# Compressed keys, values and queries as one product of 1024 columns, three of eight blocks with seven products, in one written sequence with its neighbours

## The chip, the cores and the metric

One core of one Trainium2 chip runs the whole program. The metric is the time of one execution on the device in microseconds (us). Three runs of the kernel before took 1565.64, 1566.04 and 1566.29 us, so the median is 1566.04. The execution that the profiler recorded took 1566.54 us, and its trace spans 1564.8 us. Engines are named as the profile names them: PE multiplies matrices, PEld loads its weights, DVE and ACT do the elementwise work, POOL is the third vector engine, SP issues most transfers.

## What is computed

One residual block of an encoder over 256 tokens of 2048 channels, in float32. The part that matters here is the projection of the normalised input `u` onto the columns of `w_in`, and what its compressed parts feed:

```python
def _mixer(u, positions, w_in, ...):
    proj = u @ w_in
    (r_q, r_k, r_v, r_g, c_q, c_kv, k_pe, g_ret, g_mla) = jnp.split(proj, offs, axis=-1)
    ...                                     # retention branch from r_q, r_k, r_v, r_g
    y_ret = ry @ w_ret_o
    q = (_rmsnorm(c_q, q_a_norm_g) @ w_q_b).reshape(B, S, MLA_HEADS, MLA_QK_DIM)
    q_nope, q_pe = q[..., :QK_NOPE], _rope(q[..., QK_NOPE:], positions)
    kv = (_rmsnorm(c_kv, kv_a_norm_g) @ w_kv_b).reshape(B, S, MLA_HEADS, QK_NOPE + V_HEAD)
    k_nope, v = kv[..., :QK_NOPE], kv[..., QK_NOPE:]
    k_pe = _rope(k_pe.reshape(B, S, 1, QK_ROPE), positions)
    ...                                     # block-causal attention of 16 heads
    y_mla = my.reshape(B, S, MLA_V_W) @ w_mla_o
    merged = jax.nn.sigmoid(g_ret) * y_ret + jax.nn.sigmoid(g_mla) * y_mla
    return merged @ w_out
```

`c_q` and `c_kv` have 512 columns each, `k_pe` has 64, and each gate `g_ret`, `g_mla` has 2048. After the mixer comes a feed-forward part of 8192 hidden channels, which the change leaves alone.

## The kernel before

**Numbers in two halves.** Every float32 weight and activation is split into `hi`, a rounded copy that ACT casts, and `lo`, the rest that DVE subtracts (`split`, L548 to L551, and `weights`, L162 to L170). A product then takes three matmuls: hi by hi, hi by lo and lo by hi. Each matmul has 128 by 128 weights (tokens) against up to 512 columns. All of this work, from loading (`raw` tiles, 512 KB each, a ring of five) to the cast, the subtraction and the matmuls, is a stream: SP loads, ACT and DVE prepare, PE multiplies.

**Blocks with eight and with seven products.** The large products `gr` (the gate `g_ret`), `yr` (`w_ret_o`) and `gm` (the gate `g_mla`) come from `product` (L484). Their 2048 columns are done in two halves of 1024 columns, and each half runs over eight blocks of 256 input channels (`KP` is 8). A plain block (`Eight`) has two parts of 4 products, so 24 matmuls of 512 columns. A block by Strassen's scheme in Winograd's form (`Seven`) has four parts of 2, 2, 2 and 1 products, so 21 matmuls, and DVE first builds weight sums `fa` and `fb` for it (L307, L316, L317) that also have to be split. `SEVEN` says which of the eight blocks are of this kind, for each half.

**Banks.** A half of a product fills all eight banks of PSUM: four that both kinds of block add to (`ROLE`), and four that only `Seven` blocks use. PSUM has two pools of four banks, `mmps` and `atps`; `Banks.add` gives `ROLE` banks one pool and the others the other pool, by turns from half to half. After the last `Seven` of a half `partial` (L444) folds its own four banks into `tmp` with two ACT copies and four DVE operations; after the last block `done` adds these sums to the four `ROLE` banks.

**What sets the order.** `stream` (L470) writes the order out by hand: at part n it loads up to part n+6, prepares up to part n+4, does the matmuls of part n, then calls `after(n)` and whatever stands in `later` (`soon`). Every engine takes its instructions in this order. The ring of prepared weights has six slots (four `hi`/`lo` pairs and two more). Work outside such a written sequence is ordered by an automatic scheduler.

**The stages around the change.** `gr` and `yr` are one written sequence (L894 to L906). Then, in automatic order, come `c_kv` with `k_pe` as one product of 576 columns in two pieces of 288 (tiles `kv`, `kw`, from L952) and `c_q` with 512 columns (tile `cq`, from L974), both plain. `lora_norm` squares the raw sums on ACT, takes the root on POOL and scales on DVE straight from PSUM; `lora_turn` transposes the result on PE into `cc`, cut into hi and lo. `late_turn` (L964) does the same for the key `k_pe` and turns it by its position (`rope`, L685). The second written sequence is `gm` (L992). After it the attention (tiles `lt`, `ms`, `mt`, `my`) is ordered automatically; its first products read `cc`.

Of the kernel before, what the change touches and what calls it, by code (L numbers as in the profile page):

```python
# [19 lines left out]
P = 128  # L20
S = 256
# [23 lines left out]
SEVEN = {"rv": ((2, 4, 5), (2, 4, 5)), "gr": ((3, 5), (2, 4, 5)), "yr": ((2, 4, 5), (2, 4, 5)), "gm": ((3, 5, 6), (2, 4, 5))}  # L45
# [60 lines left out]
def block_kernel(ctx: ExitStack, tc: tile.TileContext, A):  # L106
# [234 lines left out]
    class Banks:  # L341
        def __init__(self, name, half, pairs, steps):
            self.name, self.half, self.q = name, half, {}
            self.left = {f: steps for f in range(1, 8)}
            self.left[0] = 0
            for f in ROLE.values():
                self.left[f] += 2 * (pairs - steps)

        def add(self, f, a, w):
            if f not in self.q:  # L350
                self.q[f] = (mmps if (f in ROLE.values()) == (self.half == 0) else atps)(f"{self.name}{self.half}{f}")
                start = True
            else:
                start = False
# [129 lines left out]
    def product(parts, name, src, x, sets, tmp, at, done, order):  # L484
        count = sum(isinstance(p, Seven) for p, h in parts if h == 0)
        for half in range(2):
            banks = Banks(name, half, KP, len(at[half]))
# [14 lines left out]
            for m in range(KP):  # L502
# [228 lines left out]
    def tokens(out, act):  # L731
        def done(banks, t, c, col):
            o = out[:, t, col * 512 : (col + 1) * 512]
# [153 lines left out]
    yc = kp.tile([P, max(map(len, SEVEN["yr"])), 2, 4, P], F32R, name="yc")  # L887

# [4 lines left out]

    parts = product([], "gr", A["w_gret"], x, xc, tmp, SEVEN["gr"], tokens(m1, AF.Sigmoid), range(KP))  # L894
    making = iter([])

    def after(n):
# [9 lines left out]
    kctx.close()  # L907

    with ExitStack() as mctx:
        cc = big("cc", F32R, shape=(P, 2 * LT, 2, S))  # L910
        kpe = rope_pool.tile([P, S], F32, tag="kpe", bufs=1, name="kpe")
        lp = ExitStack()
        lpool = lp.enter_context(tc.tile_pool(name="lp", bufs=1))

        def lora_norm(s, parts):
            n = len(parts) // 2
            cn = lpool.tile([P, 2, LORA], F32, name=f"cn{s}")
            ss = lpool.tile([P, 2, 32], F32, name=f"ss{s}")[:, :, :n]
            for i, (t, c0, ps) in enumerate(parts):
                o = cn[:, t, c0 : c0 + ps.shape[1]]  # L920
                SC.activation(
                    o, ps, AF.Square, scale=rx[:, t : t + 1], accum_out=ss[:, t, i // 2 : i // 2 + 1]
                )
            r = lpool.tile([P, 64], F32, name=f"rc{s}")[:, :2]
            if n == 1:
                rms(r, ss[:, :, 0], LORA, 2)
            else:
                V.tensor_tensor(out=r, in0=ss[:, :, 0], in1=ss[:, :, 1], op=ALU.add)
                rms(r, r, LORA, 2)
            V.tensor_tensor(out=r, in0=r, in1=rx, op=ALU.mult)  # L930
            for t, c0, ps in parts:
                V.tensor_scalar(cn[:, t, c0 : c0 + ps.shape[1]], ps, r[:, t : t + 1], None, op0=ALU.mult)
            return cn

        def lora_turn(s, cn):
            pTs = [atps(f"lt{s}{jj}") for jj in range(2)]
            for jj, pT in enumerate(pTs):
                for j in range(2):
                    for t in range(2):
                        o = j * S + t * P  # L940
                        k = 2 * jj + j
                        PE.transpose(pT[:, o : o + P], cn[:, t, k * P : (k + 1) * P], ident)
            yield
            for jj, pT in enumerate(pTs):
                for j in range(2):
                    k = 2 * jj + j
                    g = (V_QA, V_KV)[s] + k
                    o = cc[:, LT * s + k]
                    split(o[:, 0], o[:, 1], pT[:, j * S : (j + 1) * S], scale=vec[:, g : g + 1])
            yield  # L950

        pkv = [[mmps(f"kv{t}"), mmps(f"kw{t}")] for t in range(2)]  # L952
        for k in range(0, KT, 2):
            for half in range(2):
# [3 lines left out]
        kn = lpool.tile([P, 2, 2, 64], F32, name="kn")  # L958
        for t in range(2):
            for j in range(2):  # L960
                SC.activation(kn[:, t, j], pkv[t][1][:, 224:288], AF.Copy, scale=rx[:, t : t + 1])
# [629 lines left out]
```

## Time and profile before

| what | value |
|---|---|
| time, median of three runs | 1566.04 us |
| the profiled execution: its time | 1566.54 us |
| the profiled execution: its span | 1564.8 us |
| ACT busy | 962.6 us (62%) |
| PEld busy | 1311.0 us (84%) |
| mean share of the 16 DMA engines in use, 452.4 to 500.3 us | 0.70 to 0.72 |
| granted PE clock in every stretch quoted below | 1.00 |

Engines overlap, so their busy times don't add up. The one that is never idle in a stretch sets the time of that stretch, and an engine that is idle there costs nothing. A busy PE is a modelled quantity, since matmuls are pipelined; so the pace of PE is best read as a stretch of time divided by the matmuls in it. `L357` names a line of the kernel before; the same helpers stand one to three lines further down in the changed kernel.

### The profile page before, as it was taken

The numbers are of one execution on the slowest core, as the hardware profiler recorded it, in microseconds if no ns is written. First come the engines' busy times: TensorE is split into PE (matmuls) and PEld (weight loads), VectorE is DVE, ScalarE is ACT, GpSimd is POOL, SyncE is SP. The second block draws the span as 40 slices with busy tenths as digits, with TensorE's granted clock in tenths as the row PEclk, the third lists the DMA queues.
The fourth block names the chain that finished last, engine by engine and source line by source line (L and its number), as shares of the span: only waits on it lengthen the run. The fifth ranks groups of instructions, "written<-read, shape, count | busy, mean of one in ns | idle before, by whom it ended". The sixth has DMA issues, their size and how long they took to land.

```text
span 1564.8 us, 21391 instructions
## 1 busy us (share of the span) xinstructions
PE 1551.3 (99%) x7655; PEld 1311.0 (84%) x7655; DVE 1316.0 (84%) x1787; ACT 962.6 (62%) x1416; POOL 39.3 (3%) x76
## 2 busy tenths in 40 slices
PE   9999999999999999999999999999999999999997
PEld 7888888888898888888888888888888888888886
DVE  7898877799976988976567689887978899989996
ACT  6645655566545667875445567676767766656664
POOL 0000000000000000000000000000000100000000
PEclk9999999999999999999999999999999999999999
DMA  9666755566656654444556657666675977686873
GB/s 319 207 203 208 230 164 161 159 201 206 206 168 220 213 197 143 157 136 161 185 206 211 236 196 247 214 226 232 207 249 188 376 265 245 237 304 211 266 255 115
DMA packets 107626, 333.70 MB, mean 213 GB/s; under 512 B 11264, under 2 KB 12160, under 8 KB 106496
## 3 DMA queue, kind: packets, MB, share of 16 engines
q1 hardware_dynamic: 104208, 318.71, 61.1%
q0 software_dynamic: 3168, 11.54, 1.9%
q10 hardware_dynamic: 144, 2.10, 0.4%
q8 instruction: 60, 0.98, 0.3%
q14 instruction: 46, 0.38, 0.1%
HBM read 319.72 MB, written 12.58 MB: 212 GB/s over the span
## 4 chain that ended last, share of the span: by engine, by line
PE 79%; DVE 1%; issue 1%; ACT 1%; DVEq 0%; POOLq 0%; POOL 0%; ACTq 0%
PE z L176 9%; PE dn L358 7%; PE dn L359 7%; PE dn L357 7%; PE z L180 5%; PE zs L333 2%; PE zs L334 2%; PE zs L335 2%; PE mo L214 2%; PE mo L215 2%; PE mo L217 2%; PE wo L214 2%; PE wo L215 2%; PE wo L217 2%; PE gm L357 2%; PE yr L358 2%
## 5 line engine op out<-in xcount | busy, mean ns | idle before, releaser
L551 DVE TENSOR_TENSOR lo<-raw,hi 128x1024 fp32r<-128x1024 f32 (+3 forms) x214 | 232.0, 1101 | 22.7 <-ACT hi L550 22.2
L169 DVE TENSOR_TENSOR lo<-raw,hi 128x1024 fp32r<-128x1024 f32 (+1 forms) x148 | 173.2, 1171 | 89.7 <-ACT hi L168 89.6
L168 ACT CAST hi<-raw 128x1024 fp32r<-128x1024 f32 (+1 forms) x148 | 149.6, 1011 | 155.9 <-PE mo L215 44.9
L550 ACT CAST hi<-raw 128x1024 fp32r<-128x1024 f32 (+3 forms) x214 | 200.0, 953 | 55.3 <-issue 9.5
L551 DVE TENSOR_TENSOR morelo<-raw,morehi 128x1024 fp32r<-128x1024 f32 (+1 forms) x118 | 127.1, 1098 | 18.8 <-ACT morehi L550 18.3
L550 ACT CAST morehi<-raw 128x1024 fp32r<-128x1024 f32 (+1 forms) x118 | 109.1, 949 | 10.5 <-issue 3.2
L550 ACT CAST hi<-forms 128x1024 fp32r<-128x1024 f32 x70 | 73.7, 1052 | 51.2 <-DVE forms L307 28.1
L176 PE MATMUL z<-hT,morehi 128*128 128x512 f32 x408 | 101.6, 391 | 0.0
L357 PE MATMUL dn<-hi,dd 128*128 128x512 f32 x230 | 89.6, 389 | 0.0
L359 PE MATMUL dn<-hi,dd 128*128 128x512 f32 x230 | 89.5, 389 | 0.0
L358 PE MATMUL dn<-lo,dd 128*128 128x512 f32 x230 | 89.5, 389 | 0.0
L551 DVE TENSOR_TENSOR lo<-forms,hi 128x1024 fp32r<-128x1024 f32 x70 | 85.0, 1221 | 5.3 <-ACT hi L550 4.9
L176 PEld LDWEIGHTS z<-hT,morehi 128*128 128x128 f32 x408 | 74.9, 188 | 14.4
L1266 ACT COPY hs<-z 128x512 f32<-128x512 f32 x40 | 23.5, 587 | 71.2 <-PE z L180 71.1
L357 PE MATMUL dn<-morehi,dd 128*128 128x512 f32 x156 | 60.7, 389 | 0.0
L358 PE MATMUL dn<-morelo,dd 128*128 128x512 f32 x156 | 60.7, 389 | 0.0
L359 PE MATMUL dn<-morehi,dd 128*128 128x512 f32 x156 | 60.7, 389 | 0.0
L180 PEld LDWEIGHTS z<-hT,morelo 128*128 128x128 f32 x408 | 55.6, 190 | 4.0
L176 PE MATMUL z<-hT,hi 128*128 128x512 f32 x232 | 57.9, 392 | 0.0
L180 PE MATMUL z<-hT,morelo 128*128 128x256 f32 x408 | 56.9, 282 | 0.0
L307 DVE TENSOR_TENSOR forms<-raw,sraw 128x1024 f32<-128x1024 f32 x46 | 56.1, 1219 | 0.3 <-DMA raw<-w_up_s 0.3
L358 PEld LDWEIGHTS dn<-lo,dd 128*128 128x128 f32 x230 | 43.2, 188 | 9.0
(500 smaller groups left out, 4193.9 us busy)
## 6 DMA issues: line engine op xcount, KB each, us to landing
raw<-w_down SPq DMA_DIRECT2D x106, 512.0 KB, 6.0
raw<-w_up SPq DMA_DIRECT2D x80, 512.0 KB, 5.1
raw<-w_rv SPq DMA_DIRECT2D x32, 512.0 KB, 4.8
raw<-w_rg SPq DMA_DIRECT2D x32, 512.0 KB, 4.3
raw<-w_gret SPq DMA_DIRECT2D x32, 512.0 KB, 4.4
raw<-w_ret_o SPq DMA_DIRECT2D x32, 512.0 KB, 5.0
raw<-w_gmla SPq DMA_DIRECT2D x32, 512.0 KB, 4.3
raw<-w_mla_o SPq DMA_DIRECT2D x32, 512.0 KB, 3.7
```

The costliest lines, as they stand in the source:

```text
L168: SC.copy(hi, raw)
L169: V.tensor_tensor(out=lo, in0=raw, in1=hi.bitcast(F32), op=ALU.subtract)
L176: PE.matmul(out, w[0][:, k], x.both(k0 + k), start=start and k == 0, stop=False)
L180: PE.matmul(out[:, :S], w[1][:, k], x.hi(k0 + k), start=False, stop=stop and k == n - 1)
L214: PE.matmul(out, x.hi(k0 + k, ts), w[0][:, k], start=start and k == 0, stop=False)
L215: PE.matmul(out, x.lo(k0 + k, ts), w[0][:, k], start=False, stop=False)
L217: PE.matmul(out, x.hi(k0 + k, ts), w[1][:, k], start=False, stop=stop and k == nk - 1)
L357: PE.matmul(q, ah, wh, start=start, stop=False)
L358: PE.matmul(q, ah, wl, start=False, stop=False)
L359: PE.matmul(q, al, wh, start=False, stop=self.left[f] == 0)
L550: SC.copy(hi, val)
L551: V.tensor_tensor(out=lo, in0=val, in1=hi.bitcast(F32), op=ALU.subtract)
```

## The change

The product of `c_kv` and `c_q` becomes one half of 1024 columns like those of the gates, tile `c`: `w_c` holds the 512 columns of `c_kv` and then the 512 of `c_q`, and blocks 3, 5 and 6 are `Seven` blocks. The 64 columns of `k_pe` become a part of their own, `Key`, which stands behind the second block: its hi and lo halves lie side by side as 128 weight columns, so 16 matmuls of 512 columns give all four products, already turned; `mm` then joins them on ACT and DVE. `gr`, `yr`, `c` and `gm` are one written sequence, and the automatic stretch between them is gone. The sums of `c` go to `craw` in SBUF (`compressed`), are squared by ACT there, and `norm` and `turned` follow at parts 3 to 6 of `gm`. For `gm` the first half gets its `Seven` blocks at 4, 5 and 6 instead of 3, 5 and 6, and its banks change pools (`flip`); its weights use the ring of the sequence (`kb`, `spare`) and not a pool of their own (`kc`). The last product before the attention therefore leaves its `ROLE` banks in the pool `mmps` instead of `atps`.

```diff
-SEVEN = {"rv": ((2, 4, 5), (2, 4, 5)), "gr": ((3, 5), (2, 4, 5)), "yr": ((2, 4, 5), (2, 4, 5)), "gm": ((3, 5, 6), (2, 4, 5))}
+SEVEN = {"rv": ((2, 4, 5), (2, 4, 5)), "gr": ((3, 5), (2, 4, 5)), "yr": ((2, 4, 5), (2, 4, 5)), "c": ((3, 5, 6),), "gm": ((4, 5, 6), (2, 4, 5))}
...
-        def __init__(self, name, half, pairs, steps):
+        def __init__(self, name, half, pairs, steps, parity=None):
             self.name, self.half, self.q = name, half, {}
+            self.parity = half if parity is None else parity
...
-                self.q[f] = (mmps if (f in ROLE.values()) == (self.half == 0) else atps)(f"{self.name}{self.half}{f}")
+                self.q[f] = (mmps if (f in ROLE.values()) == (self.parity == 0) else atps)(f"{self.name}{self.half}{f}")
...
-    def product(parts, name, src, x, sets, tmp, at, done, order):
+    def product(parts, name, src, x, sets, tmp, at, done, order, flip=0, extra=None, slow=2):
         count = sum(isinstance(p, Seven) for p, h in parts if h == 0)
-        for half in range(2):
-            banks = Banks(name, half, KP, len(at[half]))
+        for half in range(len(at)):
+            banks = Banks(name, half, KP, len(at[half]), (half + flip) % 2)
...
-                            later.append([2 * t + c, lambda t=t, c=c: done(banks, t, c, 2 * half + c)])
+                            later.append([slow * t + (slow > 1) * c, lambda t=t, c=c: done(banks, t, c, 2 * half + c)])
...
+                if extra and m == 1:
+                    parts.append((extra, 0))
...
+    craw = kp.tile([P, 2, 2, LORA], F32, name="craw")
+    ssc = kp.tile([P, 2, 2], F32, name="ssc")
+    rc = kp.tile([P, 2, 2], F32, name="rc")
...
+    def compressed(banks, t, c, col):
+        o, p = craw[:, t, c], banks.rest[t, c]
+        V.tensor_tensor(out=o, in0=banks.q[ROLE[t, c]], in1=p, op=ALU.add)
+
+        def square():
+            SC.activation(p, o, AF.Square, scale=rx[:, t : t + 1], accum_out=ssc[:, c, t : t + 1])
+
+        later.append([1, square])
+
+    class Key:
+        def load(self, part):
+            self.raw = wtile("raw", [P, KT, 64])
+            nc.sync.dma_start(self.raw, A["w_kpe"])
+
+        def prep(self, part):
+            self.ws = [t.rearrange("p k (j n) -> p k j n", j=2) for t in pair([P, HK, P])]
+            for i, t in enumerate(self.ws):
+                split(t[:, :, 0], t[:, :, 1], self.raw[:, i * HK : (i + 1) * HK])
+
+        def mm(self, part):
+            ps = atps("kpe")
+            for k in range(KT):
+                w = self.ws[k // HK][:, k % HK].rearrange("p j n -> p (j n)")
+                PE.matmul(ps, w, x.both(k), start=k == 0, stop=k == KT - 1)
+            a, b = (rope_pool.tile([P, S], F32, tag="join", bufs=2, name=f"key{i}") for i in range(2))
+            lo, hi = slice(0, 64), slice(64, P)
+            SC.copy(a[lo], ps[lo, S:])
+            SC.copy(b[lo], ps[hi, :S])
+            V.tensor_tensor(out=a[lo], in0=ps[lo, :S], in1=a[lo], op=ALU.add)
+            V.tensor_tensor(out=a[lo], in0=a[lo], in1=b[lo], op=ALU.add)
+            V.tensor_tensor(out=a[lo], in0=a[lo], in1=rxb[lo], op=ALU.mult)
+            SC.copy(a[hi], a[lo])
+
+            def turn():
+                rope(*(t.rearrange("p (o n) -> p o n", o=1) for t in (kpe, a)), *tabs[1], 32)
+
+            later.append([2, turn])
+
+    def norm(c):
+        rms(rc[:, c], ssc[:, c], LORA, 2)
+        V.tensor_tensor(out=rc[:, c], in0=rc[:, c], in1=rx, op=ALU.mult)
+        for t in range(2):
+            V.tensor_scalar(craw[:, t, c], craw[:, t, c], rc[:, c, t : t + 1], None, op0=ALU.mult)
+
+    def turned(c):
...
+        def cut():
+            for jj, pT in enumerate(pTs):
+                for j in range(2):
+                    k = 2 * jj + j
+                    g = (V_QA, V_KV)[s] + k
+                    o = cc[:, LT * s + k]
+                    split(o[:, 0], o[:, 1], pT[:, j * S : (j + 1) * S], scale=vec[:, g : g + 1])
+
+        later.append([1, cut])
...
+    product(parts, "yr", A["w_ret_o"], ry, yc, tmp, SEVEN["yr"], gated, range(KP))
+    product(parts, "c", A["w_c"], x, xc, tmp, SEVEN["c"], compressed, range(KP), 0, Key(), 1)
+    begin = len(parts)
+    product(parts, "gm", A["w_gmla"], x, xc, tmp, SEVEN["gm"], tokens(lambda: late("gm", shape=(P, 2, D)), AF.Sigmoid), range(KP), 1)
...
-    run(product(parts, "yr", A["w_ret_o"], ry, yc, tmp, SEVEN["yr"], gated, range(KP)), after)
+        if n - begin in (3, 4):
+            norm(n - begin - 3)
+        if n - begin in (5, 6):
+            turned(n - begin - 5)
+
+    run(parts, after)
...
-        pkv = [[mmps(f"kv{t}"), mmps(f"kw{t}")] for t in range(2)]
...
-                w = weights(A["w_ckv"][k // 2, half], [P, 2, 288])
-                for t in range(2):
-                    n_tile(pkv[t][half][:, :288], w, x, t, k, 2, k == 0, k == KT - 2)
...
-            w = weights(A["w_cq"][k // 2], [P, 2, 512])
-            for t in range(2):
-                n_tile(pcq[t], w, x, t, k, 2, k == 0, k == KT - 2)
-            if k == 2:
-                late_turn()
...
-        kctx, kp, tmp = room("kc", 2, False)
...
+        "w_c": _s_steps(np.concatenate([s_ckv, s_cq], axis=1)),
+        "w_kpe": np.ascontiguousarray(s_kpe.reshape(KT, P, 64).transpose(1, 0, 2)),
```

Where the instructions stand is told at three places. The first is DVE at the change from `yr` to the compressed products. Before (`m` is the gated sum of `yr`, `lo` the weight halves of `kv` and `kw`):

```order
L891 TENSOR_TENSOR kbsums<-yr_3732,kbsums 128x512
L169 TENSOR_TENSOR lo_4074<-raw_4072,hi_4073 128x576
L892 TENSOR_TENSOR m_2705<-m_2705,kbsums 128x512
L891 TENSOR_TENSOR kbsums<-yr_3736,kbsums 128x512
L892 TENSOR_TENSOR m_2705<-m_2705,kbsums 128x512
L891 TENSOR_TENSOR kbsums<-yr_3740,kbsums 128x512
L169 TENSOR_TENSOR lo_4092<-raw_4090,hi_4091 128x576
L169 TENSOR_TENSOR lo_4110<-raw_4108,hi_4109 128x576
L892 TENSOR_TENSOR m_2705<-m_2705,kbsums 128x512
L891 TENSOR_TENSOR kbsums<-yr_3744,kbsums 128x512
L169 TENSOR_TENSOR lo_4128<-raw_4126,hi_4127 128x576
L892 TENSOR_TENSOR m_2705<-m_2705,kbsums 128x512
```

Now, from the last gated sum of `yr` on (`kbforms` are the weight sums of a `Seven` block, here block 3 of `c`; `kpe` on the right is the bank of `Key`):

```order
L905 TENSOR_TENSOR m_2705<-m_2705,kbsums 128x512
L307 TENSOR_TENSOR kbforms<-raw_4073,raw_4074 128x1024
L554 TENSOR_TENSOR lo_4115<-raw_4074,hi_4114 128x1024
L316 TENSOR_TENSOR kbforms<-kbforms,raw_4074 128x512
L317 TENSOR_TENSOR kbforms<-kbforms,raw_4073 128x512
L554 TENSOR_TENSOR spare<-kbforms,spare 128x1024
L935 TENSOR_TENSOR key_4151<-kpe,key_4151 64x256
L936 TENSOR_TENSOR key_4151<-key_4151,key_4152 64x256
L937 TENSOR_TENSOR key_4151<-key_4151,rxb 64x256
L554 TENSOR_TENSOR spare<-kbforms,spare 128x1024
L554 TENSOR_TENSOR lo_4178<-raw_4073,hi_4177 128x512
```

What moved: in the place of subtractions of 576 columns stands the preparation of a `Seven` block, and the join of the key stands inside it, ahead of its last two subtractions.

The second is ACT at the same place, now:

```order
L553 CAST hi_4114<-raw_4074 128x1024
L553 CAST spare<-kbforms 128x1024
L933 COPY key_4151<-kpe 64x256
L934 COPY key_4152<-kpe 64x256
L938 COPY key_4151<-key_4151 64x256
L553 CAST spare<-kbforms 128x1024
L553 CAST hi_4177<-raw_4073 128x512
L553 CAST hi_4204<-raw_4159 128x1024
```

Before, there were only weight casts here:

```order
L168 CAST hi_4253<-raw_4252 128x576
L168 CAST hi_4271<-raw_4270 128x576
L168 CAST hi_4289<-raw_4288 128x576
L168 CAST hi_4307<-raw_4306 128x576
L168 CAST hi_4347<-raw_4346 128x1024
L168 CAST hi_4365<-raw_4364 128x1024
```

What moved: two copies out of the key's bank, and a third that needs DVE's join, stand ahead of the casts of block 3's second sum and of block 4.

The third is DVE at the start of `gm`, ahead of its first `Seven` block. Before (`cn` is the scaled `c_q`, read from PSUM):

```order
L649 TENSOR_SCALAR rc_4568<-ss_4565 128x2
L930 TENSOR_TENSOR rc_4568<-rc_4568,rx 128x2
L932 TENSOR_SCALAR cn_4564<-cq_4344,rc_4568 128x512
L932 TENSOR_SCALAR cn_4564<-cq_4345,rc_4568 128x512
L551 TENSOR_TENSOR lo_4581<-raw_4532,hi_4580 128x1024
L551 TENSOR_TENSOR morelo_4_4585<-raw_4534,morehi_4_4584 128x1024
L551 TENSOR_TENSOR morelo_5_4589<-raw_4574,morehi_5_4588 128x1024
L307 TENSOR_TENSOR kcforms<-raw_4576,raw_4577 128x1024
L551 TENSOR_TENSOR lo_4606<-raw_4577,hi_4605 128x1024
L316 TENSOR_TENSOR kcforms<-kcforms,raw_4577 128x512
L317 TENSOR_TENSOR kcforms<-kcforms,raw_4576 128x512
L551 TENSOR_TENSOR lo_4634<-kcforms,hi_4633 128x1024
```

Now (`ssc` and `rc` hold the sums of squares and their roots for both compressed parts, `craw` the sums in SBUF):

```order
L652 TENSOR_SCALAR rc<-ssc 128x2
L947 TENSOR_TENSOR rc<-rc,rx 128x2
L949 TENSOR_SCALAR craw<-craw,rc 128x512 x2
L307 TENSOR_TENSOR kbforms<-raw_4449,raw_4450 128x1024
L554 TENSOR_TENSOR lo_4494<-raw_4450,hi_4493 128x1024
L316 TENSOR_TENSOR kbforms<-kbforms,raw_4450 128x512
L317 TENSOR_TENSOR kbforms<-kbforms,raw_4449 128x512
L652 TENSOR_SCALAR rc<-ssc 128x2
L947 TENSOR_TENSOR rc<-rc,rx 128x2
L949 TENSOR_SCALAR craw<-craw,rc 128x512 x2
L554 TENSOR_TENSOR spare<-kbforms,spare 128x1024 x2
L557 SCALAR_TENSOR_TENSOR cc<-lt_4531,vec,cc 128x256 x2
```

What moved: two norms instead of one stand in `gm`, one ahead of block 4's preparation and one in the middle of it, and the cuts into `cc` follow for both parts.

More of the change, by code (lines that the diff above doesn't have):

```diff
@@ L732, in done @@
         def done(banks, t, c, col):
[L733 removed]
+            o = (out() if callable(out) else out)[:, t, col * 512 : (col + 1) * 512]
             V.tensor_tensor(out=o, in0=banks.q[ROLE[t, c]], in1=banks.rest[t, c], op=ALU.add)
@@ L887, in block_kernel, with late @@
     yc = kp.tile([P, max(map(len, SEVEN["yr"])), 2, 4, P], F32R, name="yc")
+    kpe = rope_pool.tile([P, S], F32, tag="kpe", bufs=1, name="kpe")
+    craw = kp.tile([P, 2, 2, LORA], F32, name="craw")
+    ssc = kp.tile([P, 2, 2], F32, name="ssc")
+    rc = kp.tile([P, 2, 2], F32, name="rc")
+    lazy = {}
+    def late(name, *args, **kw):
+        if name not in lazy:
+            lazy[name] = big(name, *args, **kw)
+        return lazy[name]
     def gated(banks, t, c, col):
```

82 lines of the change are left out of this document (10 added, 72 removed).

## The prediction

> **What bounds the kernel now.** I read the page first, then the windows of the stages around the change, then the waits of PE.
>
> ```profile
> span 1564.8 us, 21391 instructions
> PE 1551.3 (99%) x7655; PEld 1311.0 (84%) x7655; DVE 1316.0 (84%) x1787; ACT 962.6 (62%) x1416; POOL 39.3 (3%) x76
> ```
>
> PE is busy for 99% of the span, so only two things can move the time: PE's own work, and waits that are put into it. The windows (columns: stretch, its length, busy time of PE, PEld, DVE, ACT and POOL, granted clock, DMA share, GB/s) show `yr`, `kv` and `kw`, `cq`, `gm`, and the start of the attention:
>
> ```profile
> 369.60:452.40 82.80, 82.80 (x367) 68.53 (x366) 74.42 (x84) 43.93 (x50) 0.00 (x0) 1.00 0.59 185
> 452.40:477.40 25.00, 25.00 (x193) 24.96 (x192) 16.33 (x23) 12.81 (x21) 0.00 (x0) 1.00 0.72 217
> 477.40:500.30 22.90, 22.90 (x109) 19.03 (x108) 16.35 (x26) 12.32 (x24) 0.69 (x1) 1.00 0.70 223
> 500.30:584.30 84.00, 84.00 (x376) 69.65 (x375) 74.79 (x87) 50.92 (x63) 0.69 (x1) 1.00 0.61 201
> 584.30:640.00 55.70, 53.86 (x318) 47.16 (x318) 49.69 (x115) 44.44 (x109) 0.32 (x1) 1.00 0.47 152
> ```
>
> PE has no idle time from 369.6 to 584.3. DVE is the second engine: 90% busy in `yr`, 89% in `gm`, but only 68% in the two plain products between (32.7 of 47.9 us). That slack is what the change spends.
>
> **PE's work.** `yr` gives the pace of 512 columns: 82.80 us over 366 matmuls (6 blocks of 21, 10 of 24) is 0.226 us each. The 288-column matmuls took 25.00 us for 192, so 0.130 each. `cq` is 96 of 512 columns, 21.7 us, and the remaining 1.2 us are 10 transposes at 0.12. Removed: 25.0 + 21.7 = 46.7 us. Added: three blocks of 21 and five of 24 are 183 matmuls, 41.4 us, and the key's 16 are 3.6, together 45.0. The 16 transposes of the two norms stay, the two of the key go (0.2). So PE's work falls by 1.9 to 2.1 us; I take 2.0. [...] The rows say 130 and 226, and they are used.
>
> **DVE's work, step by step.** The prices are read off starts that follow each other without a gap (columns: start, busy us, engine, line, operation, idle before and what ended it):
>
> ```profile
> 410.07 0.68 DVE L891 TENSOR_TENSOR kbsums<-yr,kbsums 128x512 f32<-128x512 f32 x1
> 411.40 1.22 DVE L307 TENSOR_TENSOR kbforms<-raw,raw 128x1024 f32<-128x1024 f32 x1
> 450.76 0.69 DVE L891 TENSOR_TENSOR kbsums<-yr,kbsums 128x512 f32<-128x512 f32 x1 [3.45 <-PE yr L359]
> 537.98 1.41 DVE L448 TENSOR_TENSOR kcsums<-gm,kcsums 128x512 f32<-128x512 f32 x2
> 539.30 1.22 DVE L551 TENSOR_TENSOR lo<-raw,hi 128x1024 fp32r<-128x1024 f32 x1
> 548.00 0.69 DVE L734 TENSOR_TENSOR gm<-gm,kcsums 128x512 f32<-128x512 f32 x1
> 548.60 1.22 DVE L551 TENSOR_TENSOR lo<-kcforms,hi 128x1024 fp32r<-128x1024 f32 x1
> 556.23 1.22 DVE L307 TENSOR_TENSOR kcforms<-raw,raw 128x1024 f32<-128x1024 f32 x1
> 562.85 1.22 DVE L307 TENSOR_TENSOR kcforms<-raw,raw 128x1024 f32<-128x1024 f32 x1
> 569.48 2.35 DVE L551 TENSOR_TENSOR morelo<-raw,morehi 128x1024 fp32r<-128x1024 f32 x2
> 571.75 2.35 DVE L551 TENSOR_TENSOR lo<-raw,hi 128x1024 fp32r<-128x1024 f32 x2
> ```
>
> A block with seven products costs DVE 562.85 - 556.23 = 6.6 us and PE 21 x 0.226 = 4.75; it loses 1.9. A plain block costs 2.3 against 5.4; it gains 3.2. Two of the sums in `partial` are 1.3, a gated sum of `yr` is 1.33, a sum of `c` or `gm` 0.6, one subtraction of 1024 columns 1.14.
>
> Start at 450.76, where DVE waited for the end of `yr` with four parts of `c` prepared. Ahead of the key's join stand four gated sums (5.3), the key's split (1.2), block 2 (2.3), the first part of block 3 (3.6) and one more subtraction (1.1): 464.3. PE is done with the key at 452.4 + 4 x 2.71 + 3.6 = 466.9. So DVE waits 2.6 us there, with its next five parts queued behind, and then for ACT's two copies.
>
> ```profile
> 496.92 1.73 DVE L691 TENSOR_TENSOR rope<-pk,sin 32x256 f32<-32x256 f32 x4
> L1015 DVE TENSOR_TENSOR vkp<-kpe,vkp 64x256 fp32r<-64x256 f32 x2 | 0.8, 417 | 0.0
> L1009 ACT CAST vkp<-kpe 64x256 fp32r<-64x256 f32 x2 | 0.8, 402 | 0.0
> ```
>
> One copy (0.4), three joins of 64 rows (1.2), the third copy and a cast of 1 us on ACT bring DVE to its next subtraction at 470.1. The rest of block 3 (1.7), the turn (1.7 and two operations of 0.4), block 4 (2.3), block 5 (6.6) and block 6 up to its second part (4.9) end at 488.1. PE needs that part at 466.9 + 5.4 + 4.75 + 5.4 + 4.75 + 1.4 = 488.6. I count no stall in `c`, with 0.5 us to spare.
>
> On from there: the rest of block 6 (1.7), block 7 and `gm`'s block 0 (4.5), `partial` (2.6), blocks 1 to 3 (6.8), four sums of `c` (2.4), and about 0.4 of waiting for ACT, which has four squares in front: 506.7. Now the norms and the cuts, which the trace has once in this place:
>
> ```profile
> 501.50 0.17 DVE L649 TENSOR_SCALAR rc<-ss 128x2 f32<-128x2 f32 x1 [0.94 <-ACT cn L921]
> 502.66 1.41 DVE L932 TENSOR_SCALAR cn<-cq,rc 128x512 f32<-128x512 f32 x2
> 26.63 0.49 DVE L640 TENSOR_SCALAR ang<-ang 128x256 f32<-128x256 f32 x2
> L845 DVE TENSOR_SCALAR on<-ro,mv,rsd 128x256 f32<-128x256 f32 x16 | 8.0, 540 | 4.4 <-POOL rsd L843 4.4
> 512.13 0.48 DVE L554 SCALAR_TENSOR_TENSOR cc<-lt,vec,cc 128x256 fp32r<-128x256 f32 x1
> 514.57 0.48 DVE L554 SCALAR_TENSOR_TENSOR cc<-lt,vec,cc 128x256 fp32r<-128x256 f32 x1 [0.54 <-ACT cc L553]
> ```
>
> A norm's root takes DVE 502.66 - 501.50 = 1.2, since it waits for POOL. Scaling two tiles took 1.41 from PSUM; now the source is SBUF, where two operations of 256 columns take 0.49 together, so 0.4 for each of 512 is nearer: 0.8. [...] A cut is 512.13 to 515.05, 2.9 us, because ACT and DVE take turns. Two norms (4.0), two cuts (5.8) and block 4 (6.6) end at 523.1, block 5 at 529.7, block 6 up to its second part at 534.6. PE starts `gm` at 488.6 + 3.4 + 5.4 = 497.4 and needs this part after four plain blocks (21.7), 16 transposes (1.9), two blocks (9.5) and 1.4, at 532.0. DVE is 2.6 us late, so PE stalls for 2.6 in all over these blocks. How near this was before:
>
> ```profile
> 530.41 1.22 DVE L551 TENSOR_TENSOR morelo<-kcforms,morehi 128x1024 fp32r<-128x1024 f32 x1
> 534.04 0.39 PE L357 MATMUL gm<-morehi,xc 128*128 128x512 f32 x1
> ```
>
> The same part of the same block was ready at 531.6 and used at 534.0, 2.4 us early. Afterwards five plain parts give DVE its lead back before block 2 of the second half, and I count no further stall.
>
> **What costs nothing, and why.** The bytes stay as they were, and the loads (4.3 us from issue to landing for `w_gmla`) are issued six parts ahead; only block 5 of `c` is near, whose second load waits for block 3's buffer until 471.8 and lands at about 476, when DVE gets to it at 476.6. If that cover is gone it adds its delay to the 2.6. The attention starts with the same work in another order; DVE has as much ahead of the first scores (tile `ms`, for which PE waited 1.0 us) as before, so I take 0.
>
> ```profile
> raw<-w_gmla SPq DMA_DIRECT2D x32, 512.0 KB, 4.3
> PE ms L1022 <- DVE k L541: 1.0, 1, 1.0
> ```
>
> **The sum.** -2.0 of PE's work and +2.6 of stall make +0.6. On the profiled execution, 1566.54 us, that is 1567.1; it ran 0.5 above the median of the three runs, so against the median 1566.6 us. The bounds of the stall are 0 (DVE's sum is 84 us long, and 3% less work ends it) and 3.8 with scaling at the PSUM price (two times 0.6 more), so 1564.0 to 1567.8.
>
> **The rivals.**
>
> No stall: DVE does the small operations faster than I count. For it: PE never waited here before, at 89 to 90% DVE. Against it: the key's wait of 2.6 us comes on top, and block 4, 5 and 6 in a row lose 5.6 us of lead. 1566.04 - 2.0 = 1564.0; if the attention also loses its 1.84 us of idle time, 1562.2.
>
> Slower: DVE waits for ACT's casts inside the long run from 467 to 534, where it has no lead to pay with.
>
> ```profile
> DVE lo L551 <- ACT hi L550: 8.5, 11, 1.5
> DVE spare L551 <- ACT spare L550: 2.7, 4, 1.0
> ```
>
> In 283 to 590 these were 11.2 us, so 3.1 in 84 us at the same rate. Against it: many of them fell where the ring was full and cost nothing. The place is block 6 of `gm`; the stall would be 5.7 and the time 1566.04 - 2.0 + 5.7 = 1569.7. It decides from 2.5 us of such waits on.
>
> The attention: its order is new on all engines for some 60 us, with DVE at 49.69 of 55.70. If the idle time there triples, +3.7 and 1570.3 with the forecast's stall. That PE has less to do is not open: its order has 53 rows fewer.
>
> **Chances.** A measurement of this kernel tells about 0.2% (3.1 us) from no change. The forecast, stall of 1 to 4.5 us and so 1565 to 1568.5: 0.48. No stall: 0.22, of which 0.08 lie under 1562.9. Waits for ACT: 0.24, over 1569.2. Attention: 0.06, likewise. So faster 0.08, same 0.48 + 0.14 = 0.62, slower 0.30. The range from 1563.2 to 1570.5 leaves out most of the 0.08 and the far ends of the last two; the forecast's own is 1564.0 to 1568.5.
>
> **What would show it.** PE's work: 183 matmuls on tile `c` at 0.226 us in 41 to 42 us, and 3.6 for the key. The stall: PE waits for DVE in blocks 5 and 6 of `gm`'s first half, 2.6 us together, and none in `c`; DVE busy without a gap from about 470 to 540. The key: DVE idle for some 3 us before its join at 467. Wrong would be: PE waits in `c`, or of over 1 us at the first products of the attention, or none at all in `gm`.

## The result, and the profile after

The changed kernel took 1570.55 us (median of 8 runs, 1569.20 to 1571.72) against 1565.89 for the kernel before beside it: a ratio of 1.003, interval 1.0019 to 1.0041. It is slower, by 4.5 us against the 1566.04 of the prediction, and 0.05 us above the end of the range. The profiled execution is its shortest, 1569.2 us.

The page, and then the windows of the four stages (columns as before). The last three are cut at the first matmul of `c`, `gm` and the attention; the first begins 0.83 us behind the first matmul of `yr`, which stands at 368.81:

```profile
span 1567.4 us, 21193 instructions
PE 1550.7 (99%) x7564; PEld 1305.1 (83%) x7564; DVE 1331.8 (85%) x1804; ACT 967.5 (62%) x1413; POOL 39.1 (2%) x76
```

```profile
369.64:451.77 82.13, 82.13 (x364) 67.99 (x363) 76.36 (x85) 47.48 (x53) 0.00 (x0) 1.00 0.64 211
451.77:497.01 45.24, 45.24 (x201) 37.27 (x199) 39.80 (x49) 22.32 (x27) 0.00 (x0) 1.00 0.51 156
497.01:585.88 88.87, 86.23 (x384) 69.96 (x383) 80.56 (x101) 54.31 (x73) 1.38 (x2) 1.00 0.61 204
585.88:640.00 54.12, 50.90 (x293) 44.29 (x292) 47.90 (x105) 43.48 (x104) 0.31 (x1) 1.00 0.50 153
```

The two traces do not start alike: up to `c`, everything stands 0.83 us earlier here than in the trace before (the first matmul of `rv` at 97.35 instead of 98.18). Times of two traces are therefore compared below by their distance from the first matmul of a stage.

`c` takes 45.24 us without a gap, and `gm` has 2.64 us of idle PE that it did not have. What PE waited for in these stages (total us, times, longest):

```profile
PE lt L199 <- DVE k L544: 2.5, 2, 2.2
PE gm L359 <- DVE lo L554: 1.5, 2, 0.8
PE lt L199 <- DVE q L544: 0.7, 1, 0.7
PE gm L358 <- DVE cc L557: 0.7, 2, 0.5
PE gm L359 <- DVE spare L554: 0.4, 1, 0.4
```

The timeline of PE shows the last wait in `gm` and the longest of the attention:

```profile
534.43 0.40 PE L358 MATMUL gm<-hi,xc 128*128 128x512 f32 x1
535.63 0.50 PE L359 MATMUL gm<-lo,xc 128*128 128x512 f32 x1 [0.80 <-DVE lo L554]
...
598.98 0.64 PE L201 MATMUL lt<-cc,lo 128*128 128x256 f32 x4
601.77 0.47 PE L199 MATMUL lt<-cc,hi 128*128 128x512 f32 x1 [2.16 <-DVE k L544]
```

From start to start, the first of these two waits costs 1.20 - 0.23 = 0.97 us, not the 0.80 that is shown as idle; the matmul after it takes 0.50 instead of 0.39.

The stages of all kernels that ran, from the first matmul of one stage to that of the next in the profiled executions (`wo` is the product behind the attention), beside the median time of all runs and its difference to the kernel before on the same chip. The start (97.2 to 98.2 us up to the first matmul of `rv`) differs between executions of one kernel; `rv` to `yr` and the stages behind `wo` agree within 0.6 us in all.

| kernel | `yr` to `gm` | `gm` | attention to `wo` | sum, against before | median | against before |
|---|---|---|---|---|---|---|
| before | 130.84 | 83.88 | 203.03 | 417.75 | 1566.04 | |
| after | 128.20 | 88.87 | 204.06 | +3.38 | 1570.55 | +4.66 |
| again | 128.26 | 88.47 | 205.61 | +4.59 | 1571.70 (one run) | +5.63 |
| key_late | 128.14 | 87.99 | 204.09 | +2.47 | 1569.10 | +3.03 |
| c_one | 129.43 | 86.00 | 204.88 | +2.56 | 1569.23 | +3.16 |
| lt_swap | 128.25 | 88.44 | 204.44 | +3.38 | 1569.98 | +3.91 |
| hide | 128.22 | 86.02 | 204.11 | +0.60 | 1566.73 | +0.43 |
| ckv_late | 128.22 | 90.80 | 203.45 | +4.72 | 1572.05 | +5.75 |
| gm_two | 128.25 | 85.71 | 203.72 | -0.07 | 1567.58 | +1.28 |
| lt_pool | 128.25 | 88.81 | 201.53 | +0.84 | 1566.63 | +0.33 |
| all_three | 128.12 | 86.01 | 201.54 | -2.08 | 1564.05 | -1.98 |
| act_scale | 128.14 | 87.94 | 201.54 | -0.13 | 1565.70 | -0.24 |
| before_pool | 130.85 | 83.87 | 200.42 | -2.61 | 1563.49 | -2.54 |
| before_pool2 | 130.85 | 83.87 | 200.36 | -2.67 | 1563.11 | -2.83 |

So the change won 2.6 us up to `gm` (1.0 of it only moved: eight of the transposes now stand in `gm`), lost 5.0 in `gm` and 1.0 in the attention. That is 3.4 us. The medians differ by 4.5 us (4.66 on the same chip); the rest, 1.1 to 1.3 us, is in no stage of the profiled execution, but in those of others.

### The profile page after: what moved, and what is told of

It reads as the page before. It is cut to its first block, busy times and chain, and to the rows that moved or that the text cites. A ratio compares the mean times of both kernels' runs of the same rounds, so it can differ in the third digit from the quotient of the medians.

```text
span 1567.4 us, 21193 instructions
## 1 busy us (share of the span) xinstructions
PE 1550.7 (99%) x7564; PEld 1305.1 (83%) x7564; DVE 1331.8 (85%) x1804; ACT 967.5 (62%) x1413; POOL 39.1 (2%) x76
## 4 chain that ended last, share of the span: by engine, by line
PE 77%; DVE 3%; issue 1%; ACT 1%; POOL 0%; DVEq 0%; POOLq 0%; ACTq 0%
PE z L176 9%; PE dn L360 7%; PE dn L358 7%; PE dn L359 7%; PE z L180 5%; PE zs L333 2%; PE zs L334 2%; PE zs L335 2%; PE mo L217 2%; PE mo L214 2%; PE mo L215 2%; PE wo L215 2%; PE wo L214 2%; PE wo L217 2%; PE yr L358 2%; PE yr L359 2%
## 5 line engine op out<-in xcount | busy, mean ns | idle before, releaser
L554 DVE TENSOR_TENSOR lo<-raw,hi 128x1024 fp32r<-128x1024 f32 (+3 forms) x229 | 248.8, 1103 | 22.8 <-ACT hi L553 22.1
L553 ACT CAST hi<-raw 128x1024 fp32r<-128x1024 f32 (+3 forms) x230 | 214.9, 955 | 59.2 <-PE yr L360 8.7
L169 DVE TENSOR_TENSOR lo<-raw,hi 128x1024 fp32r<-128x1024 f32 x124 | 151.5, 1222 | 74.2 <-ACT hi L168 73.7
L168 ACT CAST hi<-raw 128x1024 fp32r<-128x1024 f32 x124 | 130.4, 1052 | 127.1 <-PE mo L215 39.2
L554 DVE TENSOR_TENSOR morelo<-raw,morehi 128x1024 fp32r<-128x1024 f32 (+1 forms) x107 | 115.0, 1096 | 17.7 <-ACT morehi L553 17.2
L553 ACT CAST morehi<-raw 128x1024 fp32r<-128x1024 f32 (+1 forms) x107 | 98.7, 947 | 9.3 <-PE dn L360 2.7
L360 PEld LDWEIGHTS dn<-hi,dd 128*128 128x128 f32 x230 | 43.2, 188 | 9.0
```

The source lines that it names most:

```text
L168: SC.copy(hi, raw)
L169: V.tensor_tensor(out=lo, in0=raw, in1=hi.bitcast(F32), op=ALU.subtract)
L360: PE.matmul(q, al, wh, start=False, stop=self.left[f] == 0)
L553: SC.copy(hi, val)
L554: V.tensor_tensor(out=lo, in0=val, in1=hi.bitcast(F32), op=ALU.subtract)
```

## The experiments

In the expectations, TensorE, VectorE, ScalarE and GpSimd are PE, DVE, ACT and POOL.

**again**: the changed kernel, nothing edited.

> The changed kernel as it is, a second profile. If the profiled execution is typical, PE waits for DVE in blocks 4 to 6 of gm's first half (some 3.9 us with the restarts) and for DVE at the first products of the attention (some 3 us), as in the first profile, and the time is 1569 to 1572. If the extra 1 to 2 us that most runs show over the first profile have one place, this profile shows a longer wait there.

1571.70 us, with the same waits. Its attention is 1.5 us longer than in the first profile. The windows of 2 us (after PEld, DVE, ACT and POOL stands the granted clock) show where, and the timeline of PE shows what it does to the matmuls:

```profile
602.00:604.00 2.00, 1.76 (x6) 1.51 (x7) 1.91 (x7) 1.39 (x5) 0.00 (x0) 0.69 0.66 238
604.00:606.00 2.00, 2.00 (x12) 2.00 (x11) 2.00 (x4) 1.85 (x5) 0.00 (x0) 0.50 0.40 147
606.00:608.00 2.00, 2.00 (x13) 1.82 (x13) 1.82 (x10) 0.41 (x1) 0.00 (x0) 0.96 0.30 74
```

```profile
602.24 1.60 PE L199 MATMUL lt<-cc,hi 128*128 128x512 f32 x4 [2.16 <-DVE k L544]
603.63 1.06 PE L201 MATMUL lt<-cc,lo 128*128 128x256 f32 x4
```

After the wait of 2.16 us PE's clock is halved (0.50) for some 3.4 us: four matmuls take 1.60 us, while the four behind the same wait in the first profile, where the clock stayed at 1.00, took 1.16.

**key_late**: the key's copies and joins stand two parts later (and its turn later still).

```diff
-            SC.copy(a[lo], ps[lo, S:])
...
-            later.append([2, turn])
+            later.extend([[2, copies], [2, joins], [5, turn]])
```

> The changed kernel, but the join of the key is written two parts later (its turn five), so that DVE does not stand before it while PE still multiplies. Theory, DVE's lateness sets the stall and the key's hold is 4.9 us of it (3.35 and 1.54 idle): DVE comes to gm that much earlier, the waits in gm's first half fall from 3.9 us to under 1, and the time is 1566.5 to 1568. Rival, the stall comes from the burst itself (three blocks with seven products in a row behind two norms and two cuts) and the key's hold is hidden: the waits stay at 3 us or more and the time at 1569.5 to 1571.

1569.10 us, ratio 1.0021 (1.0013 to 1.0030), between the two times that were expected. DVE reached the first norm 55.1 us behind the first matmul of `c` instead of 56.0 (506.69 and 507.80 in the two traces), and `gm` became 0.9 us shorter. The 3.35 and 1.54 us that DVE idles at the key are thus mostly paid back before `gm`, where DVE had slack.

**c_one**: one block of `c` with seven products instead of three (the entry of `c` in `SEVEN`).

```diff
-"c": ((3, 5, 6),)
+"c": ((3,),)
```

> The changed kernel, but c has one block with seven products (block 3) and seven plain ones: PE has 6 matmuls more (1.4 us), DVE 8.6 us less to do. Theory, DVE is the bound from 467 to 536: no wait is left in gm's first half (-3.9), so 1570.5 + 1.4 - 3.9 = 1568, less or more by what the attention's new order does. Rival, PE's work sets the time and the waits are not DVE's load: 1572.

1569.23 us, ratio 1.0021 (1.0012 to 1.0030). PE has 1.2 us more to do in `c`, so it gets to `gm` later. DVE, spared 8.6 us, is only 1.7 us earlier at the norm (54.4 us behind the first matmul of `c` instead of 56.0), and waits for others ahead of it:

```profile
502.67 1.23 DVE L554 TENSOR_TENSOR lo<-raw,hi 128x1024 fp32r<-128x1024 f32 x1 [1.06 <-ACT hi L553]
505.39 1.23 DVE L554 TENSOR_TENSOR spare<-raw,spare 128x1024 fp32r<-128x1024 f32 x1 [1.50 <-ACT spare L553]
506.53 0.16 DVE L652 TENSOR_SCALAR rc<-ssc 128x2 f32<-128x2 f32 x1
```

The lead that DVE can build up is limited: the written sequence lets it prepare four parts ahead. The casts on ACT that come before these subtractions wait in turn for PE's matmuls of `c`:

```profile
498.82 1.05 ACT L553 CAST hi<-raw 128x1024 fp32r<-128x1024 f32 x1 [1.66 <-PE c L360]
```

`gm` shrinks by 2.9 us, which is these two shifts; the attention ran into 3.1 us of wait in one piece, and 0.8 us of the gain is lost there.

**lt_swap**: the two halves of the first projections take the banks of the two pools the other way round.

```diff
-            ps = (atps if spare and i else mmps)(f"lt{uid[0]}{i}")
+            ps = (atps if spare and not i else mmps)(f"lt{uid[0]}{i}")
```

> The changed kernel, but the first products of the attention take their banks from the other pool (the first of a pair from atps, the second from mmps), which matches the pool in which gm now leaves its early banks; the scheduler then puts the pairs on PE nearly as before the change. Theory, part of the loss is the attention's new order (PE waits for DVE to free a bank, 3.2 us against 1.7 before): those waits fall to about those of the kernel before and the time by 1 to 2 us, to 1568.5 to 1569.5, with the waits in gm as they were. Rival, the loss is all in gm: no change, 1570 to 1571.

1569.98 us, ratio 1.0026 (1.0016 to 1.0036). The waits went to other places (0.97, 0.47, 1.09 us and smaller ones), and the attention was no shorter than before the edit. Turning the pools round does not mend it.

**hide**: the same operations, but none directly behind what it waits for.

```diff
+        for fn, m in ((norm, 3), (scaled, 4), (turned, 5)):
+            if n - begin == m:
+                fn(0)
+                fn(1)
...
-        later.append([1, cut])
+        later.extend([[1, lambda: cut(False)], [2, lambda: cut(True)]])
```

> The norms and the cuts do the same operations, but VectorE no longer waits inside them: both roots are asked for at part 3 of gm and the scaling follows a part later, and ScalarE's four copies of a cut stand a part ahead of VectorE's four operations. That takes VectorE's two waits for GpSimd (0.98 and 0.80 us) and its four for ScalarE (0.54 each) out of the stretch from 507 to 524 us, 3.9 us in all. Theory (VectorE runs without a gap from 507 on and its lateness is what TensorE waits for in gm): of TensorE's five waits in the first half at most one under 0.5 us is left, and the time falls by 2.5 to 4 us against the change, to 1565.0 to 1567. Rival (the burst of three blocks stalls TensorE whatever stands ahead of it, for VectorE or ScalarE is the pace inside the burst): the waits in blocks 5 and 6 stay at 0.7 to 0.8 us each and the time falls by under 1 us.

1566.73 us, ratio 1.0007 (0.9997 to 1.0016). The timeline of DVE in the changed kernel, and then in hide:

```profile
506.65 1.23 DVE L554 TENSOR_TENSOR lo<-raw,hi 128x1024 fp32r<-128x1024 f32 x1 [1.13 <-ACT hi L553]
507.80 0.16 DVE L652 TENSOR_SCALAR rc<-ssc 128x2 f32<-128x2 f32 x1
508.94 0.16 DVE L947 TENSOR_TENSOR rc<-rc,rx 128x2 f32<-128x2 f32 x1 [0.98 <-POOL rc L653]
...
518.77 0.87 DVE L557 SCALAR_TENSOR_TENSOR cc<-lt,vec,cc 128x256 fp32r<-128x256 f32 x2 [0.54 <-ACT cc L556]
...
524.15 1.21 DVE L307 TENSOR_TENSOR kbforms<-raw,raw 128x1024 f32<-128x1024 f32 x1
```

```profile
506.80 1.23 DVE L554 TENSOR_TENSOR lo<-raw,hi 128x1024 fp32r<-128x1024 f32 x1 [1.13 <-ACT hi L553]
...
511.87 0.88 DVE L951 TENSOR_SCALAR craw<-craw,rc 128x512 f32<-128x512 f32 x2
...
517.80 0.69 DVE L554 TENSOR_TENSOR lo<-raw,hi 128x512 fp32r<-128x512 f32 x1 [1.80 <-ACT hi L553]
518.41 3.22 DVE L970 SCALAR_TENSOR_TENSOR cc<-lt,vec,cc 128x256 fp32r<-128x256 f32 x8
521.55 1.22 DVE L307 TENSOR_TENSOR kbforms<-raw,raw 128x1024 f32<-128x1024 f32 x1
```

Block 5's preparation begins 69.5 us behind the first matmul of `c` (452.01 in this trace) instead of 72.4 (451.77), though one wait of 1.80 us for ACT has come in place of 3.9 us of small ones. Four of PE's five waits are gone, one of 0.81 is left, and `gm` is 2.9 us shorter. The rival, that the three blocks stall whatever stands ahead, falls.

**gm_two**: block 5 of `gm`'s first half with eight products (the entry of `gm` in `SEVEN`).

```diff
-"gm": ((4, 5, 6), (2, 4, 5))
+"gm": ((4, 6), (2, 4, 5))
```

> Block 5 of gm's first half is computed with eight products: 3 matmuls more on TensorE (0.7 us), 4.3 us less on VectorE between two blocks with seven. Theory (three such blocks in a row behind the norms and cuts are too much): waits in blocks 4 and 6 gone but for the bank waits of 0.2 and 0.5 us at block 4; the waits of 0.7, 0.4 and 0.8 us vanish with their restarts, some 3 us, less 0.7: 1566.5 to 1569. Rival (the waits stand where the cuts are, not where the three blocks are): waits of over 1 us remain and the time is that of the change plus 0 to 0.7 us.

1567.58 us, ratio 1.0006 (0.9996 to 1.0015). PE has no wait left in `gm` at all, the bank waits neither: 3.2 us less, with 0.7 of new work in it. Load ahead of the three blocks and the three blocks themselves are two ends of one sum.

**ckv_late**: the norm and cut of keys and values stand behind the three blocks.

```diff
-        pTs = [mmps(f"lt{s}{jj}") for jj in range(2)]
+        pTs = [(mmps if c else atps)(f"lt{s}{jj}") for jj in range(2)]
...
-        if n - begin in (3, 4):
-            norm(n - begin - 3)
-        if n - begin in (5, 6):
-            turned(n - begin - 5)
+        if n - begin in (4, 20):
+            norm(n - begin == 4)
+        if n - begin in (6, 23):
+            turned(n - begin == 6)
```

> The norm and the cut of one of the two tiles of c (keys and values) are moved behind the burst, to parts 20 and 23 of gm, with its transposes in the other four banks; 4.9 us of VectorE's work leave the stretch ahead of blocks 4 to 6. Theory (load ahead of the burst): TensorE's waits in gm's first half fall from 2.6 us to under 0.5; VectorE ends the last split of gm 5 us later than in the change, still some 2 us before TensorE needs it, so the second half shows no more than 0.5 us of waits; time 1565.5 to 1568. Rival (gm as a whole is bound by VectorE, which has no gap from 509 to 580 us): the waits come back in the second half, in its blocks 2 to 5, with 2 us or more, and the time stays at 1568.5 to 1571.

1572.05 us, ratio 1.0036 (1.0022 to 1.0049). The waits in the first half fell from 2.6 to 0.6 us, as the theory had it. But the moved transposes waited 3.3 us, in one piece, for the `gm` sums that free their banks:

```profile
PE lt L960 <- DVE gm L737: 3.3, 1, 3.3
```

The mean granted clock of its six runs is 0.996 to 0.998, that of the changed kernel's eight 0.997 to 0.999. Whether the load alone could be moved there is left open.

**lt_pool**: all first projections of the first group, not three pairs alone, alternate between the two pools.

```diff
-                for i, ps in lora_pair(A["w_qn"][g, :, js], cq, g == jj == 0):
+                for i, ps in lora_pair(A["w_qn"][g, :, js], cq, g == 0):
...
-                for i, ps in lora_pair(A["w_kn"][g, :, js], ckv, g == jj == 0):
+                for i, ps in lora_pair(A["w_kn"][g, :, js], ckv, g == 0):
```

> Only the banks of the first projections of the attention change: all pairs of the first group alternate between the two pools of banks, not the first three pairs alone. Theory (in the change TensorE waits 0.7, 2.2 and 0.3 us there for banks that VectorE's joins of the earlier pairs still hold): with banks of both pools the waits on the joins fall below 1 us together, and the time falls by 1.5 to 2.5 us against the change. Rival (VectorE's order of work decides, in which the joins stand behind splits of weights and the rotation, and TensorE gets to the scores early instead): the waits move to other tiles of the attention, of the same size, and the time moves by less than 0.7 us.

1566.63 us, ratio 1.0001 (0.9992 to 1.0011): 2.5 us in the attention, and some 1.4 more in the median. The long wait is gone, and the ten times lie between 1565.49 and 1567.44. The matmuls that had waited read `cc` and a weight, neither of which a join writes, and with banks of both pools they do not wait: what PE waits for there is a bank. The edit is not one of banks alone, since the scheduler now also puts the products `v` ahead of the scores.

**all_three**: hide, key_late and lt_pool together.

> The changed kernel with three edits at once: VectorE's waits inside the norms and cuts hidden (hide), the key's copies and joins two parts later (key_late), and all first projections of the attention alternating between both pools of banks (lt_pool). Theory (the three stalls are separate and were all that the change lost): of TensorE's waits from 451 to 640 us none over 0.6 us is left, the profiled span is 1561.5 to 1563.5 us, no halved clock is seen after the attention's start, and the time is 1563 to 1565, that is 1 to 3 us under the kernel before: what the prediction counted as TensorE's saved work. Rival (VectorE is the bound of this stretch and gives back later what it is spared here): new waits of over 1 us appear at other tiles between 545 and 660 us and the time stays at 1566 or above.

1564.05 us, ratio 0.9987 (0.9978 to 0.9996): 2.0 us under the kernel before, as the theory had it, though one wait is over its 0.6 us. What PE still waits for in the two stages:

```profile
PE gm L359 <- DVE lo L554: 0.8, 1, 0.8
PE lt L199 <- DVE q L544: 0.6, 1, 0.6
```

The gains of hide and lt_pool add up; key_late adds nothing to hide (86.01 and 86.02 us in `gm`).

**before_pool**, and once more **before_pool2**: the kernel before with the edit of lt_pool.

> The kernel before with the edit of lt_pool alone: all first projections of the attention alternate between both pools of banks. It tells whether the 3 to 4 us that lt_pool gave belong to the change. Theory (the wait for banks there is one that the change made, by turning round which pool gm's second half holds to its end): the kernel before gains at most its own 1.84 us of idle time between 584 and 640 us, so 1564.5 to 1566.3. Rival (the two pools in alternation are better in any case): it gains 3 us or more, under 1563.3, and the change would then be slower by as much as it was.

> before_pool once more, on the chip of act_scale, so that the two are timed side by side: 1563.2 to 1563.8. If the change with all its stalls mended is worth TensorE's saved work (1.5 us between the start of c and the start of the attention), act_scale should be 0.5 to 1.5 us faster than this one; if it is not, the saved work is given back in the attention (in all_three TensorE's intervals there sum to 0.7 us more above its pace than in before_pool).

1563.49 and 1563.11 us, ratios 0.9984 (0.9975 to 0.9993) and 0.9981 (0.9972 to 0.9991). The kernel before gains 2.6 us in the attention, as much as the change does, and more than its 1.84 us of idle time. Yet it had no wait for a bank there: its two waits were for the scores (`ms`, 1.0 us, shown in the prediction) and for this one, and both are gone.

```profile
PE my L584 <- DVE pp L551: 0.7, 1, 0.7
```

So the wait of 2.16 us for a bank came with the change, but alternating pools help both kernels by the same amount. These are the shortest times of all: the change with its stalls mended (all_three) does not beat them.

**act_scale**: all_three, with ACT scaling the sums of `c`.

```diff
-            V.tensor_scalar(craw[:, t, c], craw[:, t, c], rc[:, c, t : t + 1], None, op0=ALU.mult)
+            SC.activation(craw[:, t, c], craw[:, t, c], AF.Copy, scale=rc[:, c, t : t + 1])
```

> all_three with one more edit: the scaling of the four tiles of c by the norms' roots goes from VectorE (0.4 us each) to ScalarE (0.7 each by the squares of the same tiles). It takes 1.6 us of VectorE's work away from ahead of the one wait that all_three has left in gm, 0.80 us in block 6. Theory (VectorE's load ahead of the burst is what is left): that wait vanishes with its restart, 1 us, and the time is 1562.7 to 1563.6. Rival (ScalarE's casts are needed in time by VectorE's subtractions, and 2.8 us more on ScalarE at part 4 hold them up): VectorE shows more waits for ScalarE between 508 and 520 us, the wait in block 6 stays or grows, and the time is 1564 to 1566.

1565.70 us, ratio 0.9999 (0.9990 to 1.0008), 2.6 us slower than before_pool2 beside it. DVE in that kernel:

```profile
515.23 2.37 DVE L554 TENSOR_TENSOR spare<-kbforms,spare 128x1024 fp32r<-128x1024 f32 x2 [3.56 <-ACT spare L553]
519.60 0.69 DVE L554 TENSOR_TENSOR lo<-raw,hi 128x512 fp32r<-128x512 f32 x1 [2.00 <-ACT hi L553]
```

DVE was spared 1.6 us and waits 5.6 for casts that ACT makes later, where it waited 2.4 in all_three. The rival was right. The place of the scaling costs as well as its 2.6 us of work: ACT stands idle for DVE's `rc`, with the casts behind it.

```profile
511.70 2.56 ACT L955 ACTIVATE craw<-craw,rc 128x512 f32<-128x512 f32 x4 [4.21 <-DVE rc L953]
```

## Why the prediction was wrong

**PE's work** was forecast 2.0 us lower. It is 2.64 lower up to `gm`, and the eight moved transposes give back some 1.0: 1.6. Right in kind, 0.4 too much.

**DVE up to the key, and no stall in `c`**: right in kind. DVE idles before the join at 467.26 and takes up its subtractions again at 470.12, and PE has no gap in `c`. That 470.1 was forecast is chance, since this trace stands 0.83 us earlier: behind the first matmul of `c` (452.4 in the forecast, 451.77 here) it is 18.35 us instead of 17.7. The 0.65 us come from ACT's copies: the sum has one of them ahead of the join, and the join waits for both.

```profile
467.26 0.42 DVE L935 TENSOR_TENSOR key<-kpe,key 64x256 f32<-64x256 f32 x1 [3.35 <-ACT key L934]
...
470.12 1.23 DVE L554 TENSOR_TENSOR spare<-kbforms,spare 128x1024 fp32r<-128x1024 f32 x1 [1.54 <-ACT spare L553]
```

**The stall in `gm`**: right mechanism, mis-sized term. It was put at 2.6 us, a part needed at 532.0 and ready at 534.6, which is 79.6 and 82.2 us behind the first matmul of `c`. It was ready after 83.9 us (535.63), and would have been needed after 79.8, since `gm` began after 45.24 us and not after 45.0. The difference is 4.0 us, and by 4.0 us `gm` grew beyond its transposes. Of the 1.7 us by which DVE was later than forecast, 0.65 are those of the key. The others came in ahead of the first norm, which began after 56.0 us instead of 54.3 (507.80, forecast at 506.7), at one line of the sum: "about 0.4 of waiting for ACT, which has four squares in front: 506.7". That wait was 1.13, behind squares of 0.71 us each in a run of ACT without a gap from 500.85 on; and the steps of that line make 506.5, not 506.7. The prices behind it, POOL's answer and the cuts' turns with ACT, held: from the first norm to the end of block 4 it is 16.35 us (507.80 to 524.15) against 16.4.

What was not seen is that these prices need not be paid, as hide shows, and that two of the waits come earlier, at block 4, since the transposes borrow banks of the pool that its sums need. They are gone in hide and key_late; in the sum they only let PE arrive later for the next.

**The attention, taken at 0**, is the step that failed outright. It rested on DVE having "as much ahead of the first scores" as before. A wait of over 1 us at the first products of the attention was also among the prediction's signs of being wrong, and it is there with 2.16 us. PE does not wait for the scores there, but for banks that DVE's joins free, and DVE has two splits of weights, part of the rotation and the joins of `q` in front of the join that frees them:

```profile
597.48 0.75 DVE L544 TENSOR_TENSOR q<-lt,join 128x256 f32<-128x256 f32 x2
598.14 1.21 DVE L169 TENSOR_TENSOR lo<-raw,hi 128x1024 fp32r<-128x1024 f32 x1
599.27 0.68 DVE L701 TENSOR_TENSOR pe<-pe,rope 128x512 f32<-128x512 f32 x1
599.88 1.21 DVE L169 TENSOR_TENSOR lo<-raw,hi 128x1024 fp32r<-128x1024 f32 x1
601.01 0.28 DVE L554 TENSOR_TENSOR qs<-q,qs 128x128 fp32r<-128x128 f32 x1
601.21 0.41 DVE L544 TENSOR_TENSOR k<-lt,join 128x256 f32<-128x256 f32 x1
```

In the kernel before, the first join of `k` stands ahead of both splits:

```profile
596.75 0.42 DVE L541 TENSOR_TENSOR k<-lt,join 128x256 f32<-128x256 f32 x1
597.08 1.22 DVE L169 TENSOR_TENSOR lo<-raw,hi 128x1024 fp32r<-128x1024 f32 x1
598.21 0.68 DVE L698 TENSOR_TENSOR pe<-pe,rope 128x512 f32<-128x512 f32 x1
598.82 1.22 DVE L169 TENSOR_TENSOR lo<-raw,hi 128x1024 fp32r<-128x1024 f32 x1
```

Behind the attention's first matmul (584.36 before, 585.88 now) it began after 12.4 us, and now after 15.3. The stage became 1.03 us longer. That much stays also with alternating pools (201.54 in all_three, 200.42 in before_pool); a wait of 0.55 us that before_pool does not have is in it, and the rest is open.

**The clock** was in no term. Kernels without a wait of over 2 us have medians within about 0.5 us of what their stages say (last columns of the table), while after and gm_two, whose profiles have the wait of 2.16 us at a mean granted clock of 0.999 and 0.998, lie 1.3 and 1.4 above; key_late and hide, with the same wait, lie 0.6 above and 0.2 below. Behind such a wait a halved clock is seen in the trace of again (0.50 for 3.41 us), whose mean granted clock is 0.997. For the executions without a trace there is that mean alone, from which one such stretch would take 0.5 x 3.41 / 1568 = 0.0011. In hide six runs stand at 1566.29 to 1566.81 us with 0.998 or 0.999, and four at 1568.08 to 1568.62, three of them with 0.997. In lt_pool and all_three no run is under 0.998. In the changed kernel 0.997 belongs to the longest run, 1571.72, but 1570.27 has 0.999, as the profiled 1569.20 has. So a halved clock may be a part of what the median has above the stages; how large a part stays open.

Together: -1.6 + 4.0 + 1.0 make 3.4 us, and about 1.1 of the 4.5 lies between executions.

**The rivals.** "Slower: DVE waits for ACT's casts" named most of what the sum lacked, but at other places (at the key and ahead of the norms, not in block 6) and with some 1.3 us more, not 3.1. "The attention" had the place, and 1.0 us instead of 3.7. "No stall" is excluded.

## What to carry to other kernels

An operation that waits for another engine should stand one part behind what it waits for: this alone gave 2.8 us in the stages, with the same operations. Where a written sequence limits how far an engine may run ahead, sum up its load from the point at which the lead is capped, not from the start of the stretch: c_one freed 8.6 us ahead of it and moved the norm by 1.7. And try a mend on the kernel before too: of the 5.5 us that the stages won back here, 2.6 could be had without the change.

## What the runs showed of the hardware

A wait of 2.16 us of PE was followed by half the clock (0.50) for 3.41 us in again, and not in after, where the same wait stands and the clock is 1.00 from 585.88 to 640.00 us. In again it cost some 1.5 us (its attention of 205.61 us against 204.06 in after), over half as much as the wait itself. The stretch of again that holds the wait, and the one behind it:

```profile
599.34:602.76 3.42, 1.26 (x8) 0.97 (x7) 3.39 (x8) 1.53 (x6) 0.00 (x0) 1.00 0.46 143
602.76:606.17 3.41, 3.41 (x15) 3.20 (x14) 3.35 (x8) 2.60 (x8) 0.00 (x0) 0.50 0.46 167
```

PE is idle for 2.16 of the first 3.42 us, at a clock of 1.00, and busy throughout the 3.41 us at 0.50. Why the same wait was followed by half the clock in one execution and not in the other is open.

Two kernels have a longer wait. c_one, with 3.1 us, was profiled at a mean granted clock of 0.997, as again was; ckv_late, with 3.3 us, at 0.998; after at 0.999. With shorter waits the clock was 1.00 in the stretches read here: in `gm` of after (497.01 to 585.88 us), where the longest is 0.80 us, and in the kernel before from 584.30 to 640.00 us, where it is 1.00 us.
